# Attention by head pair in a one-core transformer kernel: two half-array matmuls side by side, index scores from stacked parts

## The chip, the core and the metric

The kernel runs on one core of a Trainium2 chip. TensorE (PE in the profile) does all matrix products and transposes; its weight loads stand apart as PEld. VectorE (DVE), ScalarE (ACT) and GpSimd (POOL) do the elementwise work, and SyncE (SP) issues most transfers. The metric is the device time of one execution in microseconds (us).

## The reference

Two transformer blocks over 512 tokens of width 1024, in fp32. Cut to what matters here:

```python
# block 1: FFN, then MLA attention (8 heads) and differential attention (4 heads of two halves), FFN, a gate
s = einsum('bhqd,bhkd->bhqk', q, k) * scale          # MLA, 96 dims a head, values 64 wide
a1 = softmax(q1 k1 * scale + bias); a2 = softmax(q2 k2 * scale + bias)   # halves of 64 dims
o = (a1 - lam * a2) @ v
# block 2, over 16 meta tokens and the 512: stick-breaking attention (8 heads) and sparse attention (8 heads)
s_idx = relu(einsum('bqhd,bkd->bqhk', qi, ki))       # 8 index heads of 64 dims share one key
score = einsum('bqh,bqhk->bqk', wi, s_idx)           # then the 128 best admissible keys of each query
p = softmax(q k * scale, selected keys); o = p @ v   # 8 heads, 64 dims, 64-wide values
# then a mixture of 32 experts (2 per token) and a last norm
```

## The kernel before

**Layout.** Activations lie transposed, 128 features on the partitions and 512 tokens along the free axis (`T`; 528 with the meta tokens, `TK`). A pair of 64-dim heads shares one tile: head `e` of the pair is rows `64e` to `64e+63`. Most products are made from two parts of each operand: `HL` holds a high part and a low part in fp32r, and `mm3` makes a product of three matmuls (high by high, high by low, low by high). Attention weights and values are multiplied as plain fp32; each such matmul stands in the trace as two records.

**Stages.** In order of time: FFN 1, the mixer of block 1 (`block1`), FFN 2, the gate, the mixer of block 2 (`mixer2`, `mixer2_out`), the experts. In both mixers two generators are merged by `merge`: `attention()` and a stream of projection tasks, each of which loads a weight tile (`wload`: transfer, high part on ACT, low part on DVE or POOL in turn) and runs a chain of full-array products. Each `yield` carries a planned cost, and `merge` advances whichever generator is behind in the ratio of its two weights (100 to 135 in block 1, 115 to 180 in block 2). `need(key)` holds attention back until the stream has come to a task. The planned costs set the program order alone; the library's scheduler then orders each engine's instructions by priority and by when it takes their inputs to be ready. `next_to` pins an instruction behind the one traced before it on its engine. PE takes its instructions in the order so made.

**Attention in block 1.** `diff_s(h)` (score matmuls of the two halves of a head, in rows 0 to 63 and 64 to 127, for four blocks of 128 queries; DVE adds the bias and takes the minimum, L751, ACT the exponential, L755), `diff_o`, `mla_s(p)`, and `mla_o(p)`: for each of four key blocks and both heads of pair `p`, `cols` transposes the weights into PSUM and copies them to `at`, and one fp32 matmul (L869) adds into 64 rows of `po`.

**Attention in block 2.** `idx` makes the index scores: `prep(c)` rotates and splits the queries of two heads, `products(c)` multiplies them by the index key `ki`, whose 64 rows lie twice on the partitions; ACT takes the relu, DVE the weighted sum. `sb_a`, `sb_b` and their kin are the stick-breaking heads, `rank` steps the top-k on DVE; none of these is touched. `ds_s(p)` makes the scores of the sparse heads, one head after the other, over 144, 272, 400 and 528 keys (the last in two segments of 264), and `ds_o(p)` their products with the values, for five key blocks and each head in turn (L1505, L1515).

**Buffers.** PSUM has three pools that rotate: `G` (3 banks, accumulation), `PS` (3, scores), `PT` (2, transposes). In SBUF, `U` takes from a pool of 41 or, for names in `SHORT` (`at`, `sb`, `sbb` among them), of 27 buffers.

## Time and profile before

| | us |
|---|---|
| median of 3 runs | 2258.01 (2257.05 to 2260.27) |
| the profiled execution, its own time | 2262.45 |
| its span, first to last instruction | 2260.6 |
| mean granted TensorE clock in it | 0.975 of 2.4 GHz |

The span is that of one execution taken by the profiler; times of stretches are read from it, in us from its start. A group's "busy" is the union of its instructions, and ends of matmuls are modelled, so the cost of a matmul is read here from its start to the start of the next one.

### The profile page before, as it was taken

To read this page: it belongs to the slowest core of one execution; us is meant where nothing else is said; L and a number is where in the kernel's file an instruction comes from. 1 tells how busy PE (TensorE), PEld (TensorE's weight loads), DVE (VectorE), ACT (ScalarE), POOL (GpSimd) and SP (SyncE) were. 2 spreads that over 40 slices of the span, in tenths; PEclk is the share of its full clock that TensorE was granted. 3 is DMA by queue.
4 is the path that set the end of the run, shared out by engine and by line. 5 is a ranking of instruction groups with operands and counts; after the bars stand their busy time and mean duration, and the time that the engine had idled before them with its cause. 6 is when DMAs were issued, how large, how long until landed. Compare 5 with 4: busy or idle time off the path is not lost.

```text
span 2260.6 us, 25763 instructions
## 1 busy us (share of the span) xinstructions
PE 2188.1 (97%) x10265; PEld 1544.3 (68%) x10265; DVE 1013.9 (45%) x1715; ACT 708.3 (31%) x1173; POOL 516.9 (23%) x336
## 2 busy tenths in 40 slices
PE   8999999999899999999989899999999999999997
PEld 6888888776655788888776777755788544455543
DVE  4323235556664542433574896543363232233322
ACT  4222224444443422222342555533232111111112
POOL 3323234232220432323432344210122000000000
PEclk9999999998999999999987999999999999999999
DMA  4333224210010233232321111111534799999993
GB/s 158 98 96 94 93 93 147 71 60 29 10 47 19 89 98 94 94 93 94 119 75 47 38 38 38 42 38 47 214 100 168 296 407 410 413 403 407 413 407 156
DMA packets 67838, 330.74 MB, mean 146 GB/s; under 512 B 7792, under 2 KB 8960, under 8 KB 43648
## 3 DMA queue, kind: packets, MB, share of 16 engines
q1 hardware_dynamic: 66848, 327.45, 39.1%
q8 instruction: 83, 1.36, 0.2%
q10 hardware_dynamic: 864, 1.57, 0.2%
q14 instruction: 43, 0.35, 0.0%
HBM read 326.90 MB, written 2.10 MB: 146 GB/s over the span
## 4 chain that ended last, share of the span: by engine, by line
PE 87%; DVE 7%; ACT 2%; issue 2%; POOL 1%; DMA 1%; SPq 0%; DVEq 0%; POOLq 0%; ACTq 0%
PE psg L391 10%; PE psg L392 10%; PE psg L393 10%; PE pss L1678 10%; PE psg L1678 7%; PE pss L391 5%; PE pss L393 5%; PE pss L392 5%; PE pst L1678 4%; PE pst L392 4%; PE pst L391 4%; PE pst L393 4%; PE psg L869 1%; PE psg L1515 1%; PE pst L1035 1%
## 5 line engine op out<-in xcount | busy, mean ns | idle before, releaser
L372 ACT ACTIVATE whl<-wraw 128x1024 fp32r<-128x1024 f32 (+1 forms) x227 | 237.1, 1044 | 664.6 <-PE psg L393 258.0
L375 POOL TENSOR_TENSOR whl<-wraw,whl 128x1024 fp32r<-128x1024 f32 (+1 forms) x114 | 271.3, 2379 | 685.8 <-ACT whl L372 509.4
L375 DVE TENSOR_TENSOR whl<-wraw,whl 128x1024 fp32r<-128x1024 f32 (+1 forms) x113 | 156.9, 1388 | 55.2 <-ACT whl L372 55.1
L1978 POOL TENSOR_TENSOR fr<-fv,mhalf 128x1 f32<-128x1 f32 x4 | 2.2, 546 | 518.7 <-DVE fv L1977 516.2
L1678 PE MATMUL pss<-mw,xe 128*64 128x512 f32 x512 | 115.3, 592 | 0.0
L1678 PE MATMUL pss<-mw,hT 128*64 128x512 f32 x480 | 108.0, 603 | 0.6 <-ACT hT L1856 0.5
L1678 PE MATMUL psg<-mw,xe 128*64 128x512 f32 x480 | 108.1, 592 | 0.0
L497 POOL TENSOR_TENSOR t<-t,t 128x512 f32<-128x512 f32 x44 | 58.4, 1326 | 216.8 <-DVE t L496 199.3
L496 DVE TENSOR_TENSOR t<-pss,rb_f 128x512 f32<-128x512 f32 x44 | 30.4, 691 | 163.2 <-PE pss L393 163.2
L524 DVE SCALAR_TENSOR_TENSOR h<-pst,h 128x512 f32<-128x512 f32 x48 | 33.2, 691 | 135.1 <-PE pst L393 135.0
L1838 DVE SCALAR_TENSOR_TENSOR mt<-pss,sc,mt 128x512 f32<-128x512 f32 x16 | 12.0, 750 | 178.5 <-PE pss L1678 178.5
L1951 DVE TENSOR_TENSOR h<-h,psg 128x512 f32<-128x512 f32 x120 | 81.1, 685 | 22.7 <-PE psg L1678 22.7
L1678 PEld LDWEIGHTS pss<-mw,xe 128*64 128x64 f32 x512 | 36.8, 137 | 73.1 <-issue 73.1
L1678 PEld LDWEIGHTS psg<-mw,xe 128*64 128x64 f32 x480 | 34.4, 137 | 68.1 <-issue 65.0
L387 DVE SCALAR_TENSOR_TENSOR yel<-pss,sc,yeh 128x512 fp32r<-128x512 f32 x32 | 24.0, 751 | 122.0 <-ACT yeh L386 122.0
L1678 PEld LDWEIGHTS pss<-mw,hT 128*64 128x64 f32 x480 | 33.5, 138 | 63.9 <-issue 59.3
L1678 PE MATMUL pst<-disp,uhh 128*128 128x256 f32 x256 | 69.6, 295 | 2.9 <-DVE disp L1756 2.9
L1678 PE MATMUL pst<-disp,uhl 128*128 128x256 f32 x256 | 67.9, 289 | 0.0
L413 POOL TENSOR_TENSOR acc<-acc,sq 128x512 f32<-128x512 f32 x34 | 53.4, 1572 | 46.2 <-ACT sq L412 42.5
L1678 PEld LDWEIGHTS pst<-disp,uhh 128*128 128x128 f32 x256 | 50.4, 197 | 17.6 <-issue 13.5
L1837 ACT ACTIVATE mt<-psg,sc 128x512 f32<-128x512 f32 x16 | 11.0, 687 | 157.1 <-PE psg L1678 134.2
L386 ACT ACTIVATE yeh<-pss,sc 128x512 fp32r<-128x512 f32 x32 | 22.0, 688 | 115.6 <-PE pss L1678 103.3
(880 smaller groups left out, 5770.3 us busy)
## 6 DMA issues: line engine op xcount, KB each, us to landing
mw<-in_w SPq DMA_DIRECT2D x188, 1024.0 KB, 9.4
wraw<-in_w_gu SPq DMA_DIRECT2D x87, 512.0 KB, 3.5
wraw<-in_w_d SPq DMA_DIRECT2D x48, 512.0 KB, 3.5
wraw<-in_w2A SPq DMA_DIRECT2D x38, 512.0 KB, 3.4
wraw<-in_w_inA SPq DMA_DIRECT2D x16, 512.0 KB, 3.5
wraw<-in_w_out SPq DMA_DIRECT2D x8, 512.0 KB, 3.6
wraw<-in_w_pg SPq DMA_DIRECT2D x8, 512.0 KB, 3.6
wraw<-in_w_up SPq DMA_DIRECT2D x8, 512.0 KB, 3.5
```

Source lines behind the costliest of these rows:

```text
L372: nc.scalar.activation(hl[:, 0, :n], raw[:, :n], AF.Copy)
L375: e.tensor_sub(hl[:, 1, :n], raw[:, :n], hl[:, 0, :n].bitcast(F32))
L387: nc.vector.scalar_tensor_tensor(low, src, scale, hi.bitcast(F32), op0=OP.mult, op1=OP.subtract)
L391: mm(ps, whi, xhi, start=first, stop=False)
L392: mm(ps, whi, xlo, start=False, stop=False)
L393: mm(ps, wlo, xhi, start=False, stop=last)
L413: (eng or nc.gpsimd).tensor_add(acc, acc, t)
L496: nc.vector.tensor_tensor(t2, pu, rb, op=OP.mult)
L497: nc.gpsimd.tensor_tensor(t2, t1, t2, op=OP.mult)
L524: nc.vector.scalar_tensor_tensor(self.h[m], py, 0.5, self.h[m], op0=OP.mult, op1=OP.add)
L1678: return self.next_to(nc.tensor.matmul(*args, **kw))
L1951: self.nc.vector.tensor_tensor(self.h[m], self.h[m], ps, op=OP.add)
```

## The change

The scores of a head pair, which were two `mm3` one after the other, become `mm3_pair`: six matmuls that alternate between the two halves of the partitions, pinned one behind the other, into two `PS` banks. The value products of `mla_o` and `ds_o`, which came one by one as their `at` was copied, are gathered: `mla_o` makes four `at` and then issues the four matmuls together, and `ds_o` does so with two, from a new pool of two buffers (`AT`). Both order the two heads' matmuls next to each other, in the left and the right 64 columns of the array. The index scores no longer use half the rows: `prep` puts the high part of a head's 64 rows and its low part on the other 64 rows of one tile, so that one full-height matmul makes two of the products, and two of them (against the high and the low part of `ki`) make all, with low by low added. Planned costs change with it.

```diff
@@ -24,6 +24,7 @@
...
 NG, NS, NT, NA, NB, NW, NMA, NMB = 3, 3, 2, 41, 27, 3, 7, 5
+NAT = 2
 NX, NU = 4, 0
@@ -259,7 +260,7 @@
...
                 self.setup()
-                with tc.tile_pool(name="ub", bufs=NB, side="right") as self.ub:
+                with tc.tile_pool(name="at", bufs=NAT, side="right") as self.pa, tc.tile_pool(name="ub", bufs=NB, side="right") as self.ub:
                     self.block1()
@@ -278,6 +279,9 @@
         return (self.ub if name in SHORT else self.ua).tile([P, w], dt, name=name, tag="u")
+    def AT(self):
+        return self.pa.tile([P, 512], F32, name="at", tag="at")
     def HL(self, name, w=512):
@@ -396,6 +400,18 @@
         return self.tc.keep_in_program_order(ins)
+    def mm3_pair(self, ps, w, x):
+        mm = self.nc.tensor.matmul
+        first = True
+        for a, b in ((0, 0), (0, 1), (1, 0)):
+            for e in (1, 0):
+                ins = mm(ps[e], w(e, a), x(e, b), start=a + b == 0, stop=a == 1)
+                if not first:
+                    self.next_to(ins)
+                first = False
     def gemm(self, ps, w, xs, kc, o=0, stride=P, cols=slice(None)):
@@ -741,21 +757,21 @@
...
                 sm, es = [], []
-                for e in range(2):
-                    ps = self.PS()
-                    tk = slice(i * P, (i + 1) * P)
-                    r = slice(64 * e, 64 * e + 64)
-                    self.mm3(ps, q[r, 0, tk], q[r, 1, tk], k[r, 0, :], k[r, 1, :], True, True)
+                tk = slice(i * P, (i + 1) * P)
+                rows = [slice(64 * e, 64 * e + 64) for e in range(2)]
+                pss = [self.PS() for e in range(2)]
+                self.mm3_pair(pss, lambda e, a: q[rows[e], a, tk], lambda e, a: k[rows[e], a, :])
+                for e in (1, 0):
                     sb = self.U("sb")
                     mn = self.S("mn", 1)
-                    nc.vector.tensor_tensor_reduce(out=sb, in0=ps, in1=dist[i], op0=OP.add, op1=OP.min, scale=1.0,
+                    nc.vector.tensor_tensor_reduce(out=sb, in0=pss[e], in1=dist[i], op0=OP.add, op1=OP.min, scale=1.0,
                                                    scalar=3.0e38, accum_out=mn)
...
                     nc.scalar.activation(sb, sb, AF.Exp, bias=mn, scale=-(4.0 ** -(h + 1)), accum_out=s)
-                    sm.append(s)
-                    es.append(sb)
-                yield 1.3
+                    sm.insert(0, s)
+                    es.insert(0, sb)
+                yield 0.8
                 cf = self.S("cf", 1)
@@ -862,12 +878,20 @@
...
             vm = vd["m", p]
-            for j in range(4):
-                for e in range(2):
-                    at = self.U("at")
-                    self.cols(at, aa[e], j)
-                    mm(po[64 * e : 64 * e + 64], vm[:, j * P + 64 * e : j * P + 64 * e + 64], at, start=j == 0, stop=j == 3)
-                    yield 0.9
+            for j0 in (0, 2):
+                ats = []
+                for e in (0, 1):
+                    for j in (j0 + 1, j0):
+                        at = self.U("at")
+                        self.cols(at, aa[e], j)
+                        ats.append((e, j, at))
+                        yield 0.45
+                for n, m in enumerate((3, 1, 2, 0)):
+                    e, j, at = ats[m]
+                    ins = mm(po[64 * e : 64 * e + 64], vm[:, j * P + 64 * e : j * P + 64 * e + 64], at, start=n < 2 and j0 == 0, stop=n > 1 and j0 == 2)
+                    if n:
+                        self.next_to(ins)
+                yield 2.2
             rbh = self.U("rbh")
@@ -1258,7 +1282,10 @@
...
                 q = self.HL("qi")
-                self.split(q, y2)
+                for e in range(2):
+                    r, o = slice(64 * e, 64 * e + 64), slice(64 - 64 * e, 128 - 64 * e)
+                    nc.scalar.activation(q[r, e, :], y2[r], AF.Copy)
+                    nc.vector.tensor_sub(q[o, e, :], y2[r], q[r, e, :].bitcast(F32))
                 qi[c] = q
@@ -1268,18 +1295,18 @@
...
                         h = 2 * c + e
-                        r = slice(64 * e, 64 * e + 64)
                         rl = self.U("relu", TK)
...
                             ps = self.PS()[:, : oe - o]
-                            self.mm3(ps, q[r, 0, tk], q[r, 1, tk], ki[r, 0, o:oe], ki[r, 1, o:oe], True, True)
+                            for s in range(2):
+                                mm(ps, q[:, e, tk], ki[:, s, o:oe], start=s == 0, stop=s == 1)
                             nc.scalar.activation(rl[:, o:oe], ps, AF.Relu)
...
                             nc.vector.scalar_tensor_tensor(mk[i], rl[:, :n], wc, mk[i], op0=OP.mult, op1=OP.add)
-                        yield n * 0.00128
+                        yield n * 0.0009
             qi = {}
@@ -1464,27 +1491,26 @@
...
             sm = self.S("smm", 8)
-            al_ = []
-            for e in range(2):
-                r = slice(64 * e, 64 * e + 64)
-                al = []
-                for i in (3, 2, 1, 0):
-                    n = NK[i]
-                    tk = slice(i * P, i * P + P)
-                    sb = self.U("sbb", TK)
-                    mn = None
-                    for o, e_ in segs(n):
-                        ps = self.PS()[:, : e_ - o]
-                        self.mm3(ps, qp[r, 0, tk], qp[r, 1, tk], kh[r, 0, o:e_], kh[r, 1, o:e_], True, True)
+            al_ = [[], []]
+            rows = [slice(64 * e, 64 * e + 64) for e in range(2)]
+            for i in (3, 2, 1, 0):
+                n = NK[i]
+                tk = slice(i * P, i * P + P)
+                sb = [self.U("sbb", TK) for e in range(2)]
+                mn = [None, None]
+                for o, e_ in segs(n):
+                    pss = [self.PS()[:, : e_ - o] for e in range(2)]
+                    self.mm3_pair(pss, lambda e, a: qp[rows[e], a, tk], lambda e, a: kh[rows[e], a, o:e_])
+                    for e in (1, 0):
                         m2 = self.S("mn", 1)
-                        nc.vector.tensor_tensor_reduce(out=sb[:, o:e_], in0=ps, in1=mk[i][:, o:e_], op0=OP.add, op1=OP.min,
-                                                       scale=1.0, scalar=3.0e38 if mn is None else mn, accum_out=m2)
-                        mn = m2
-                    nc.scalar.activation(sb[:, :n], sb[:, :n], AF.Exp, bias=mn, scale=-1.0,
+                        nc.vector.tensor_tensor_reduce(out=sb[e][:, o:e_], in0=pss[e], in1=mk[i][:, o:e_], op0=OP.add, op1=OP.min,
+                                                       scale=1.0, scalar=3.0e38 if mn[e] is None else mn[e], accum_out=m2)
+                        mn[e] = m2
+                for e in (1, 0):
+                    nc.scalar.activation(sb[e][:, :n], sb[e][:, :n], AF.Exp, bias=mn[e], scale=-1.0,
                                          accum_out=sm[:, 2 * i + e : 2 * i + e + 1])
-                    al.insert(0, sb)
-                    yield n * 0.00128
-                al_.append(al)
+                    al_[e].insert(0, sb[e])
+                yield n * 0.0014
             r1 = self.S("r1m", 8)
@@ -1493,27 +1519,31 @@
...
             for j in (4, 0, 1, 2, 3):
-                for e in range(2):
-                    pc = slice(p * P + 64 * e, p * P + 64 * e + 64)
-                    pr = slice(64 * e, 64 * e + 64)
+                ats = []
+                for e in (0, 1):
                     pt = self.PT()
-                    at = self.U("at")
+                    at = self.AT()
                     if j == 4:
...
                         nc.vector.tensor_copy(at[:NM], pt[:NM])
-                        mm(po[pr], vh[4][:NM, pc], at[:NM], start=True, stop=False)
-                        yield 0.8
-                        continue
-                    nq = T - j * P
-                    for i in range(j, 4):
-                        nc.tensor.transpose(pt[:, (i - j) * P : (i - j + 1) * P], al_[e][i][:, NM + j * P : NM + j * P + P], self.ident)
-                    if e:
-                        nc.vector.tensor_copy(at[:, :nq], pt[:, :nq])
+                        ats.append((vh[4][:NM], at[:NM], 0))
                     else:
-                        nc.scalar.copy(at[:, :nq], pt[:, :nq])
-                    mm(po[pr, j * P :], vh[j][:, pc], at[:, :nq], start=False, stop=j == 3)
-                    yield 0.9 - 0.2 * j
+                        nq = T - j * P
+                        for i in range(j, 4):
+                            nc.tensor.transpose(pt[:, (i - j) * P : (i - j + 1) * P], al_[e][i][:, NM + j * P : NM + j * P + P], self.ident)
+                        if e:
+                            nc.vector.tensor_copy(at[:, :nq], pt[:, :nq])
+                        else:
+                            nc.scalar.copy(at[:, :nq], pt[:, :nq])
+                        ats.append((vh[j], at[:, :nq], j * P))
+                    yield 0.45 - 0.1 * (j % 4)
+                for e in (1, 0):
+                    v, at, o = ats[e]
+                    ins = mm(po[64 * e : 64 * e + 64, o:], v[:, p * P + 64 * e : p * P + 64 * e + 64], at, start=j == 4, stop=j == 3)
+                    if e == 0:
+                        self.next_to(ins)
+                yield 1.3 - 0.3 * (j % 4)
             rbh = self.U("rbh")
...
```

## Rows read from the trace of the kernel before

**Rows 1.** The page: the span, and busy time of each engine.

```profile
span 2260.6 us, 25763 instructions
PE 2188.1 (97%) x10265; PEld 1544.3 (68%) x10265; DVE 1013.9 (45%) x1715; ACT 708.3 (31%) x1173; POOL 516.9 (23%) x336
```

**Rows 2.** Stretches: length, busy PE, PEld, DVE, ACT, POOL, clock, DMA share, GB/s.

```profile
385.00:505.00 120.00, 119.14 (x570) 90.69 (x569) 61.08 (x154) 52.68 (x97) 34.48 (x21) 1.00 0.23 76
505.00:605.00 100.00, 88.51 (x380) 61.24 (x379) 65.66 (x156) 49.49 (x106) 30.65 (x24) 0.88 0.09 27
605.00:745.00 140.00, 133.50 (x598) 84.01 (x597) 85.44 (x138) 61.01 (x121) 27.57 (x17) 1.00 0.11 34
1195.00:1275.00 80.00, 75.52 (x329) 56.10 (x328) 48.29 (x77) 27.47 (x59) 14.37 (x8) 0.77 0.11 40
1275.00:1385.00 110.00, 100.20 (x588) 81.08 (x587) 101.23 (x266) 57.79 (x109) 49.57 (x56) 0.97 0.12 39
1440.00:1600.00 160.00, 159.84 (x684) 99.69 (x683) 69.30 (x161) 59.18 (x125) 20.96 (x10) 0.99 0.13 43
```

**Rows 3.** Timeline of PE: differential scores, two halves that happened to alternate (start, duration).

```profile
458.08 0.50 PE L392 MATMUL pss<-dkl,dqh 64*128 64x512 f32 x1
458.09 0.49 PE L391 MATMUL pss<-dkh,dqh 64*128 64x512 f32 x1
458.42 0.39 PE L393 MATMUL pss<-dkh,dql 64*128 64x512 f32 x1
458.43 0.39 PE L392 MATMUL pss<-dkl,dqh 64*128 64x512 f32 x1
458.66 0.39 PE L393 MATMUL pss<-dkh,dql 64*128 64x512 f32 x1
458.98 0.44 PE L1035 MATMUL pst<-ident,ad 128*128 128x128 f32 x2
```

**Rows 4.** Timeline of PE: one half's three score matmuls alone.

```profile
459.57 0.49 PE L391 MATMUL pss<-dkh,dqh 64*128 64x512 f32 x1
...
460.45 0.33 PE L1035 MATMUL pst<-ident,ad 128*128 128x128 f32 x1
```

**Rows 5.** Timeline of PE: one fp32 value product (two records) and what follows it.

```profile
702.75 1.07 PE L869 MATMUL psg<-at,vm 128*64 128x512 f32 x2
703.75 0.66 PE L445 MATMUL pst<-ident,bce 128*128 128x128 f32 x4
```

**Rows 6.** The chain of waits, experts: eight fp32 products (16 records), alternating column halves.

```profile
2000.86 3.43 PE pss L1678 x16
```

**Rows 7.** Timeline of PE: sparse scores of one head, 528 keys, then 400.

```profile
1512.85 0.38 PE L391 MATMUL pss<-khh,qph 64*128 64x264 f32 x1
...
1513.77 0.50 PE L391 MATMUL psg<-xs2h,whl 128*128 128x512 f32 x1
...
1515.68 0.45 PE L391 MATMUL pss<-khh,qph 64*128 64x400 f32 x1
...
1516.42 0.49 PE L391 MATMUL psg<-xs4h,whl 128*128 128x512 f32 x1
```

**Rows 8.** Stretches of the index scores, columns as in rows 2.

```profile
1210.50:1237.80 27.30, 26.48 (x69) 16.79 (x68) 11.24 (x17) 6.76 (x17) 1.65 (x2) 0.50 0.10 37
1258.20:1268.50 10.30, 10.30 (x52) 9.67 (x51) 8.56 (x22) 6.80 (x14) 1.29 (x1) 0.50 0.00 0
```

**Rows 9.** Timeline of PE: full-height matmuls of 264 columns, one behind the other.

```profile
1250.03 0.28 PE L391 MATMUL psg<-xs6h,whl 128*128 128x264 f32 x1
1250.15 0.28 PE L392 MATMUL psg<-xs6l,whl 128*128 128x264 f32 x1
```

**Rows 10.** DVE: timeline of one split; group of score passes (busy, mean ns).

```profile
1207.28 2.44 DVE L384 TENSOR_TENSOR qil<-yqi,qih 128x512 fp32r<-128x512 f32 x1 [1.54 <-ACT qih L383]
...
L751 DVE CUSTOM_DVE_ANT_0 sb<-pss,dist 128x512 f32<-128x512 f32 x32 | 21.9, 683 | 0.5 <-PE pss L393 0.4
```

**Rows 11.** Waits of PE, 385 to 745 us: total, times, longest.

```profile
PE pss L391 <- DVE mn L751: 2.1, 1, 2.1
```

## The prediction, made before the changed kernel ran

> **What bounds the kernel now.** I read the page first, then a table of stretches, then the timeline of PE inside each stretch that the change touches. The page has PE busy for 2188.1 of 2260.6 us and no other engine for half of it [rows 1]. The stretches show where that holds for the attention [rows 2]. From 385 to 505, the differential heads, PE is busy for 119 of 120 us, and from 1440 to 1600, the sparse heads, for all of 160, with DVE and ACT far below: a microsecond off PE's queue is there a microsecond off the end, as long as the projections that fill it last. From 505 to 605, where block 1 passes from differential to MLA heads, PE stands idle for 11.5 us and its clock averages 0.88: chains through DVE and ACT set part of that stretch. From 1195 to 1275, the index scores, PE is busy for 75.5 of 80 us, but at a mean clock of 0.77. From 1275 to 1385, the stick-breaking heads with the top-k, DVE is busy for 101 of 110 us; nothing of the change lies there. The experts and both FFNs, most of the span, aren't touched, so everything below is a sum over four stretches.
>
> **Scores of the differential heads.** One half's three matmuls, alone, hold PE from 459.57 to 460.45, 0.88 us: three times 0.23 us and some 0.2 us for going over to half-height matmuls and back [rows 4]. The trace shows the new form by luck: where the two halves alternate, their matmuls start 0.01 us apart, and five of the six take 0.90 us, from 458.08 to 458.98 [rows 3]. So six side by side cost what three cost now. There are 4 heads, 4 query blocks and 2 halves: 32 groups of 0.88 us are 28.2 us, 16 pairs of 0.90 us are 14.4 us. Some are interleaved already, so I take 13 us, not 13.8. If the halves did not run together, the gain would be 0; that is the lower bound.
>
> **Value products of MLA.** One fp32 product alone takes 1.00 us to the next start [rows 5]. In the experts, where the two column halves alternate, eight take 3.43 us, 0.43 us each [rows 6]; twice 0.43 from 1.00 leaves 0.14 us for entry and exit. Now 32 stand alone, 32.0 us. After, 8 groups of four cost 4 x 0.43 + 0.14 = 1.86 us, together 14.9 us. The gain is 17 us; transposes and copies of `at` stay as they are.
>
> **Value products of the sparse heads.** Per pair and head: two of 512 columns, then 384, 256 and 128. With 0.14 us fixed and 0.86 us per 512 columns, an estimate from [rows 5], that is 1.00 + 1.00 + 0.79 + 0.57 + 0.36 = 3.72 us, over 8 heads 29.8 us. A pair costs as much as one does alone, so half goes: 14.9 us, of which I take 14.
>
> **Scores of the sparse heads.** One head's 528 keys take 0.92 us and its 400 keys 0.74 us [rows 7]; shorter blocks scale to about 0.58 and 0.45 us. That is 2.69 us a head and block set, 21.5 us over 8; half is 10.8 us. The two segments of 528 now want four score banks where there are three, so some second pairs come apart; I take 10 us.
>
> **Index scores.** Three half-height matmuls become two of full height, with no going over to another mode. At the spacing of [rows 9], 0.12 us for 264 columns, one head costs 2 x (2 x 0.12 + 0.18 + 0.12 + 0.11) = 1.3 us, 10.4 us for 8; by [rows 7] the old form costs 21.5 us if every head stands alone. Heads already overlap in this stretch, so I take 7 of these 11 us. The larger item is the clock: for 27.3 and 10.3 us it was granted 0.50, the 1.2 GHz level, with PE busy for 36.8 us of it [rows 8]; at 2.4 GHz that work takes half, so 18.4 us are lost now. Half-height matmuls fill much of these stretches; before the first, PE had waited for a split on DVE that took 2.44 us [rows 10]. After, the matmuls are full-height, and the same split is two DVE instructions, so the first drop stays and the way back should be shorter. The bounds are 0 and 18 us; I take 11, nearer to the upper because the work that stays is dense. The added split instructions, one more of about 0.7 us on DVE, as a DVE pass over 512 columns takes [rows 10], and one on ACT for each of 4 head pairs, hide behind the products of the pair before, all but the first; uncovered, 1.4 us each.
>
> **What is added as waits.** A pair starts when the later of its two operands is there. Behind it on PE's queue stand the next projection matmuls, and for those wait a `G` bank's evacuation on DVE and the next weight tile. The new two-buffer pool makes the copy of key block j+1 wait for the pair of block j: about 2 us of chain per block, 20 blocks, 40 us inside a stretch of 160 that has projections to fill it. Planned costs move: attention is emitted sooner against the stream, whose weight loads on SP keep their order and only come later against attention. The new pool lies beside the one that the experts' first weight tiles will reuse; they wait for the end of attention as before.
>
> **Given back.** In 505 to 605 the chains stay; a third of the differential gain falls there, and thinner PE work means longer idle: 6 us. In 605 to 745, 3 us. In the index stretch DVE, 48 of 80 us now, comes close to PE: 3 us. In the stick-breaking stretch, where DVE sets the time, a little less projection work lies under it: 3 us. Together 15 us, an estimate between 5 and 35.
>
> **Sum.** 13 + 17 + 14 + 10 + 7 + 11 = 72 us off PE, less 15: 57 us. The profiled execution took 2262.45 us, 1.85 us more than its span; so 2205 us for one like it, and, against the median of 2258.01, 2201 us. That is 2.5% faster. About 0.2%, 4.5 us, can be told from no change.
>
> **A rule against it.** The scores of a query block are emptied from PSUM by DVE, and the two halves of one block need 2 x 0.68 us there for the pass alone [rows 10], more than the 0.90 us that PE will need [rows 3]. The Trainium skill, "TensorEngine Tiling (Array Packing)", section "Performance Considerations", says that tiling speeds up TensorE but not the emptying of PSUM, which may become the bottleneck. By that rule the first rival below would be the outcome.
>
> **Rivals.**
> *Evacuation takes over.* Within a burst of differential attention DVE then sets the step, and PE's gain counts only where projections fill it. For it: DVE is at 66 of 100 us in 505 to 605 and PE idles already [rows 2]. Against it: over all of 385 to 745 DVE has 212 of 360 us. Then block 1 keeps 10 of 30 us, the index stretch 7 of 18, the sparse heads 20 of 24: 37 us, 2221 us. Chance 0.18.
> *The clock comes back wholly and little is given back.* 72 + 7 - 5 = 74 us, 2184 us. For it: dense full-height work; against it, every new gap on PE. Chance 0.08.
> *The pairs don't run together,* because the order made for PE puts other work between them. Then only the index part is left, 18 less 3: 2243 us. Against it: rows 3 and 6 show pairs where nothing stands between. Chance 0.05.
> *Slower: pairs wait on PE's own queue.* A pair takes two of three `PS` banks, so the next waits for DVE, and pinned in order it stops all behind it. There are 16 + 8 + 20 + 20 = 64 groups. The longest wait of this kind now is 2.1 us, once [rows 11]. At 2.1 us each that is 134 us against 72: 2320 us. It decides from 72 / 64 = 1.1 us a group. Against it: projections can stand between two pairs, and only the second segment of 528 keys follows at once. Chance 0.07, of which 0.02 within 0.2%.
>
> **How the numbers follow.** My forecast has 0.62, with its own range of 2186 to 2216 us. To leave no more than 2 in 10 out, the range takes in the first rival and the better clock down to 2182 us; upwards to 2234 us. Faster: 0.62 + 0.18 + 0.08 + 0.05 = 0.93; the slower rival gives 0.02 within 0.2% and 0.05 slower.
>
> **What would show it.** Score matmuls of `dkh` and `khh` starting in twos within 0.02 us; `L869`'s successor in groups of four in about 1.9 us; PE busy in the mixer of block 1 less by about 30 us; the clock below 1 in the index stretch for well under 37 us; the sparse stretch some 22 us shorter with PE still full. Wrong would be: new PE waits on DVE or on `at` above 20 us in total, more stretches at 0.50 than before, or lone half-height matmuls.

## The result

The changed kernel takes 2198.54 us (median of 4 runs, 2197.20 to 2201.16) against 2258.65 us for the kernel before beside it: ratio 0.9735, 95% interval 0.9721 to 0.9749, so 2.65% faster. Later, on two chips, it took 2200.20 and 2199.73 us. The profiled execution took 2201.16 us and its span is 2199.3 us. The forecast was 2201 us.

The page's span, busy times of all engines, and chain of waits, after:

```profile
span 2199.3 us, 25719 instructions
...
PE 2115.3 (96%) x10225; PEld 1520.7 (69%) x10225; DVE 1012.4 (46%) x1719; ACT 707.7 (32%) x1177; POOL 517.4 (24%) x336
...
PE 83%; DVE 9%; ACT 3%; issue 2%; POOL 1%; DMA 1%; SPq 0%; DVEq 0%; ACTq 0%; POOLq 0%
```

PE is busy for 72.8 us less than in [rows 1], and the span is 61.3 us shorter: PE stands idle for 84.0 us in all (2199.3 - 2115.3) where it was 72.5. The other engines do the same work. The stretches that answer to [rows 2], moved to where the same work now lies; the first three make up the attention of block 1:

```profile
385.00:505.00 120.00, 117.09 (x579) 90.39 (x577) 61.29 (x155) 52.85 (x98) 35.66 (x22) 0.99 0.24 77
505.00:600.00 95.00, 83.60 (x397) 59.70 (x394) 65.36 (x161) 51.96 (x114) 29.65 (x23) 0.87 0.09 28
600.00:721.00 121.00, 111.92 (x578) 79.95 (x577) 83.20 (x133) 57.45 (x114) 27.95 (x17) 1.00 0.13 40
1170.00:1230.00 60.00, 53.87 (x291) 44.83 (x289) 48.42 (x75) 30.33 (x64) 15.16 (x8) 0.97 0.16 53
1230.00:1340.00 110.00, 99.17 (x578) 83.36 (x577) 103.06 (x269) 56.77 (x108) 50.52 (x55) 0.94 0.12 39
1395.00:1530.00 135.00, 132.63 (x680) 87.75 (x679) 69.34 (x164) 58.65 (x128) 18.54 (x10) 1.00 0.16 48
```

The largest single change is in the fourth line: the index scores, which took 80 us at a mean clock of 0.77, take 60 us at 0.97. In the sparse heads (last line) PE is still nearly full; in stick-breaking (fifth line) DVE is still the engine nearest to full, 103 of 110 us.

Where the 61 us came from, by starts in the timeline of PE: the second FFN of block 1 starts 24.5 us earlier than before (836.3 to 811.9), the first index matmul 22.6 (1207.4 to 1184.7), the first stick-breaking matmul 45.9 (1271.1 to 1225.1), the first output projection of block 2 62.7 (1675.3 to 1612.6), the end 61.4. So block 1 gave about 24 us and the index stretch 23; 17 more lie between the first stick-breaking matmul and the first output projection, and the FFNs and the experts gave nothing. Within these 17, the first sparse score matmul is 40.1 us earlier (1444.6 to 1404.5): 5.8 us were lost ahead of it, in and behind stick-breaking, and the sparse heads gave 22.6.

**The pairs.** Two score pairs of a differential head in PE's timeline, after:

```profile
419.17 0.51 PE L410 MATMUL pss<-dkh,dqh 64*128 64x512 f32 x2
419.51 0.40 PE L410 MATMUL pss<-dkl,dqh 64*128 64x512 f32 x2
419.74 0.39 PE L410 MATMUL pss<-dkh,dql 64*128 64x512 f32 x2
419.97 0.39 PE L410 MATMUL pss<-dkh,dqh 64*128 64x512 f32 x1
420.29 0.50 PE L395 MATMUL psg<-xs4h,whl 128*128 128x512 f32 x1
420.63 0.39 PE L396 MATMUL psg<-xs4l,whl 128*128 128x512 f32 x1
...
421.64 0.49 PE L410 MATMUL pss<-dkh,dqh 64*128 64x512 f32 x1
421.65 0.72 PE L410 MATMUL pss<-dkl,dqh 64*128 64x512 f32 x2
421.99 0.60 PE L410 MATMUL pss<-dkh,dql 64*128 64x512 f32 x2
422.23 0.39 PE L410 MATMUL pss<-dkh,dqh 64*128 64x512 f32 x1
```

The first pair runs in three twos, 0.80 us to the fourth row. That fourth row is the first matmul of the *next* pair, alone: it starts at once, so its bank, the third, was free. Its partner starts at 421.64, as the second of the two DVE passes that empty the pair before ends (the row below, 420.97 and 0.68); until then projections come between (420.29). The next pair runs staggered, and behind it the first matmul of the one after stands alone again (422.23). Of 48 twos of the differential heads 43 start within 0.03 us of each other, of 60 of the sparse heads 51.

```profile
420.97 0.68 DVE L767 CUSTOM_DVE_ANT_0 sb<-pss,dist 128x512 f32<-128x512 f32 x1
```

**The value products of MLA** come in groups of four (eight records); to the next start one group takes 1.86 us:

```profile
693.73 1.94 PE L891 MATMUL psg<-at,vm 128*64 128x512 f32 x8
695.59 0.50 PE L397 MATMUL psg<-oT7h,whl 128*128 128x512 f32 x1
```

**The clock of the index stretch.** What answers to [rows 8]: the two stretches at 0.50 are 3.4 and 6.8 us long, and between them, with PE busy for 38.6 of 44.4 us, the clock stays at 1.00. The second lies behind the last index matmul (1222.3), in stick-breaking.

```profile
1186.50:1189.90 3.40, 3.40 (x11) 3.19 (x12) 2.21 (x4) 1.72 (x4) 0.00 (x0) 0.50 0.13 53
1189.90:1234.30 44.40, 38.55 (x232) 32.51 (x231) 39.24 (x67) 27.43 (x62) 10.67 (x7) 1.00 0.11 36
1234.30:1241.10 6.80, 5.96 (x19) 5.27 (x20) 6.66 (x16) 2.23 (x4) 2.39 (x3) 0.50 0.26 77
```

### The profile page after: what moved, and what is told of

Read it like the earlier page. It is cut to its first block, busy times and chain, and to the rows that moved or that the text cites. A ratio compares the mean times of both kernels' runs of the same rounds, so it can differ in the third digit from the quotient of the medians.

```text
span 2199.3 us, 25719 instructions
## 1 busy us (share of the span) xinstructions
PE 2115.3 (96%) x10225; PEld 1520.7 (69%) x10225; DVE 1012.4 (46%) x1719; ACT 707.7 (32%) x1177; POOL 517.4 (24%) x336
## 4 chain that ended last, share of the span: by engine, by line
PE 83%; DVE 9%; ACT 3%; issue 2%; POOL 1%; DMA 1%; SPq 0%; DVEq 0%; ACTq 0%; POOLq 0%
PE pss L1708 10%; PE psg L395 9%; PE psg L397 9%; PE psg L396 9%; PE psg L1708 8%; PE pss L395 4%; PE pss L397 4%; PE pss L396 4%; PE pst L1708 4%; PE pst L396 4%; PE pst L395 4%; PE pst L397 4%; PE pss L410 1%; PE pst L479 1%; PE pst L1713 1%
## 5 line engine op out<-in xcount | busy, mean ns | idle before, releaser
L1708 PE MATMUL pst<-disp,uhl 128*128 128x256 f32 x256 | 67.5, 288 | 0.0
L429 POOL TENSOR_TENSOR acc<-acc,sq 128x512 f32<-128x512 f32 x34 | 53.5, 1573 | 46.2 <-ACT sq L428 42.5
```

What stands on the lines that cost most here:

```text
L429: (eng or nc.gpsimd).tensor_add(acc, acc, t)
L1708: return self.next_to(nc.tensor.matmul(*args, **kw))
```

## The experiments

One number is used throughout, the **time lost at 0.50** of a profiled execution: span x (1 - mean granted clock), what the span would be shorter by if PE set the time everywhere and always had 2.4 GHz. The third digit of the clock makes it uncertain by 1.1 us. What is left, span less this, is called the work below. All times are medians. The groups of runs were on different chips; the kernel before, beside each of them, took 2252.6 to 2260.2 us, and a ratio is to the one beside. The last three columns are of one execution each, and the lost time differs between executions: over all of them on record it is 49.5 to 61.1 us for the kernel before, while its work is 2198.7 to 2206.5 us. So differences in the column of lost time are safe only well above 5 us.

| kernel | us | span, clock of the profile | lost at 0.50 | work |
|---|---|---|---|---|
| before | 2258.65 | 2260.6, 0.975 | 56.5 | 2204.1 |
| changed (second profile) | 2200.20 | 2198.4, 0.982 | 39.6 | 2158.8 |
| only_index | 2239.27 | 2233.0, 0.984 | 35.7 | 2197.3 |
| only_values | 2222.22 | 2221.3, 0.978 | 48.9 | 2172.4 |
| only_scores | 2237.05 | 2233.8, 0.981 | 42.4 | 2191.4 |
| heads_in_turn | 2211.18 | 2202.2, 0.984 | 35.2 | 2167.0 |
| index_as_before | 2213.51 | 2211.7, 0.976 | 53.1 | 2158.6 |
| index_three | 2205.20 | 2203.3, 0.981 | 41.9 | 2161.4 |
| index_pair | 2210.80 | 2211.4, 0.977 | 50.9 | 2160.5 |
| four_banks | 2251.98 | 2250.5, 0.970 | 67.5 | 2183.0 |
| held_pairs | 2193.19 | 2193.9, 0.982 | 39.5 | 2154.4 |
| held_in_block1 | 2197.89 | 2197.9, 0.980 | 44.0 | 2153.9 |

**One part at a time.** Each takes the hunks of the change for that part and nothing else but the new, there partly unused, pool: `only_index` the stacked split and the two full-height matmuls; `only_values` the grouped products of `mla_o` and `ds_o`; `only_scores` `mm3_pair` in `diff_s` and `ds_s`.

> The kernel before with the index scores from stacked parts alone (the split into stacked parts, two full-height matmuls instead of three half-height ones). Theory A (the parts add up, each by what it takes off PE's queue where PE is full): about 20 us faster, 2238 us, of which most is the stretch at 0.50 that shrinks from 37 us to about 10 us, with the attention of block 1 as before. Theory B (the clock of the index stretch came back for another reason, because everything ahead of it had moved): the long stretch at 0.50 stays, and the gain is some 6 us, 2252 us.

Measured 2239.27 us, ratio 0.9925 (0.9897 to 0.9953). The stretch at 0.50 is gone, with no matmul ahead of it changed; what was the first of [rows 8] now runs at 1.00:

```profile
1207.00:1243.00 36.00, 31.49 (x185) 26.73 (x186) 31.35 (x47) 20.78 (x49) 8.37 (x5) 1.00 0.17 47
```

Theory A. By the table, 20.8 us of its gain are clock and 6.8 us work.

> The kernel before with the value products of the MLA heads and of the sparse heads grouped, and nothing else. Theory A: 16.7 us of MLA and 13.5 us of sparse products come off PE, 30 us, of which a few are given back as idle time ahead of the index stretch: 2230 us, between 2226 and 2236. Theory B (an evacuation by DVE or ACT sets the pace, and the products had been hidden behind copies of the attention weights): half of that or less, above 2240 us.

Measured 2222.22 us, ratio 0.9843 (0.9815 to 0.9870), below the range of theory A. Work gave 31.7 us, about what the products take less (30); the rest is clock by the table. Theory B, the rival of the evacuation, has nothing here.

> The kernel before with the scores of the differential and of the sparse heads by pair, and nothing else (the sparse value products take their copies from the new small pool, but one by one as before). Theory A: 9.4 and 7.0 us come off PE, 16 us, of which a little is lost again: 2245 us, between 2241 and 2250. Theory B (pairs wait on PE's own queue for a free score bank or for DVE): no gain or slower, 2256 us or more.

Measured 2237.05 us, ratio 0.9923 (0.9897 to 0.9949), a gain of 21 us and below theory A's range of times. By the table it is 12.7 us of work and 14.1 us of clock, but the profiled execution was its fastest; over all five the lost time is 42.4 to 56.1 us. No waiting of pairs on PE's queue made it slower.

The three parts gain 19, 36 and 21 us by their medians, 76 in all, where the whole change gained 60. The table shows why: in work they sum to 6.8 + 31.7 + 12.7 = 51.2 us against 45.3, nearly additive; in time lost at 0.50 they sum to 42.5 us against 16.9. Medians over all executions, each against the kernel before beside it, say the same with less spread: 2.1 + 29.0 + 12.3 = 43.4 us of work against 45.8, and 16.0 + 5.3 + 8.3 = 29.6 us lost at 0.50 against 14.7. So it looks as if each part alone recovered some of the same low stretches, which can be recovered only once.

**The heads in turn.** Everything as changed, but the alternation:

```diff
-        for a, b in ((0, 0), (0, 1), (1, 0)):
-            for e in (1, 0):
+        for e in (1, 0):
+            for a, b in ((0, 0), (0, 1), (1, 0)):
```

> The changed kernel, but in the pair of score matmuls the three matmuls of one head come first and then the three of the other; banks, pins, planned costs and all else are unchanged. Theory A (the two halves of the array run at the same time when their matmuls alternate): the 16 us that the scores gained are lost again, 2214 us, and score groups take 0.88 us a head instead of 0.90 us for both. Theory B (the gain of the scores comes from the new order and the new planned costs): within 4 us of the changed kernel, 2195 to 2203 us.

Measured 2211.18 us, 11 us above the changed kernel: theory A, a little smaller. One head alone now takes 0.87 us to the projection behind it (421.08 to 421.95), where a whole pair takes 0.90 us for both (419.41 to 420.31 in `held_pairs`, below). Summed from each start to the next start on PE, at most 1 us for each, all score matmuls take 43.8 us (before 48.9, changed 32.5). That is not all of the gain lost: some still overlap at the seam of the two heads, most of them in the sparse heads (17.0 us where the kernel before took 21.5). PE's timeline of two heads of this kernel:

```profile
421.08 0.49 PE L410 MATMUL pss<-dkh,dqh 64*128 64x512 f32 x1
421.41 0.39 PE L410 MATMUL pss<-dkl,dqh 64*128 64x512 f32 x1
421.64 0.39 PE L410 MATMUL pss<-dkh,dql 64*128 64x512 f32 x1
421.95 0.50 PE L395 MATMUL psg<-xs5h,whl 128*128 128x512 f32 x1
422.38 0.50 PE L410 MATMUL pss<-dkh,dqh 64*128 64x512 f32 x1
```

**The clock of the index stretch, three ways.** `index_as_before` undoes the index part in the changed kernel. `index_three` keeps the stacked parts but issues three full-height matmuls, counting the low part of the key twice. `index_pair` goes back to half-height matmuls, those of two heads alternating, and to the old split; the heads' weighted sum runs in another order.

The core of `index_three`, and then of `index_pair`:

```diff
-                            for s in range(2):
-                                mm(ps, q[:, e, tk], ki[:, s, o:oe], start=s == 0, stop=s == 1)
+                            for n_, s in enumerate((0, 1, 1)):
+                                mm(ps, q[:, e, tk], ki[:, s, o:oe], start=n_ == 0, stop=n_ == 2)
```

```diff
+                self.split(q, y2)
...
+                        pss = [self.PS()[:, : oe - o] for e in range(2)]
+                        self.mm3_pair(pss, lambda e, a: q[rows[e], a, tk], lambda e, a: ki[rows[e], a, o:oe])
```

> The changed kernel with the index scores and their split as they were before the change. Theory A (work adds up, but the time lost at 0.50 is shared: each part alone recovered some of the same low stretches): 7 us of matmul work come back and a stretch of 0.50 of about 20 to 27 us in the index part, 2215 to 2219 us in all; with the clock set aside (span less the time lost at 0.50), 6 to 8 us more than the changed kernel. Theory B (the parts add up in time as well): 2219 to 2221 us by the 19 to 21 us of the index part alone, with no such difference in what is lost at 0.50.

> The changed kernel with three full-height index matmuls instead of two; the third counts the low part of the key a second time. So the work of the index scores in matmuls is as it was before the change, but without half-height ones. Theory A (the half-height matmuls kept PE at 0.50 there): no stretch of 0.50 above 10 us in the index stretch, only the 7 us of the added matmuls are lost, 2205 us. Theory B (the clock came back because there is less index work, or none of it waits): a stretch of 0.50 of 20 us or more comes back, 2212 us or more.

> The changed kernel with the index scores as pairs of half-height matmuls of two heads, as in the other scores, and the old split; the heads' weighted sum runs in another order. Theory A (half-height matmuls keep the clock low, side by side or not): a long stretch of 0.50 comes back, 2207 us or more. Theory B (it is the half-filled array that keeps the clock low; pairs fill it): 0.50 stays as short as in the changed kernel, PE spends three starts on two heads instead of four, and the time is 2192 to 2199 us.

`index_as_before` took 2213.51 us, 13 us more than the changed kernel, a little less than theory A's range, and by the table all of the 13 us is clock (53.1 against 39.6 us lost; by medians of all executions 11 of them): the work, which I had expected to be 6 to 8 us more, is the same within the reading. The long stretch is back, as in [rows 8]; the matmuls saved by stacking are paid for by PE's idle time, 34.4 us from 1135 to 1700 us in the changed kernel and 28.9 us here. `index_three` took 2205.20 us, and no long stretch came back: theory A. So half as many index matmuls again leave the clock alone. `index_pair` took 2210.80 us, and two stretches of 10.2 us at 0.50 are there, though its index matmuls take PE 17.0 us from start to start, little more than the full-height ones (14.4): theory A again. The stretches of `index_as_before`, and then those of `index_pair`:

```profile
1189.00:1216.30 27.30, 26.49 (x69) 16.74 (x69) 11.24 (x17) 6.87 (x17) 1.74 (x2) 0.50 0.10 38
1236.80:1247.00 10.20, 10.20 (x52) 9.57 (x51) 8.45 (x22) 6.80 (x14) 1.28 (x1) 0.50 0.00 1
```

```profile
1188.70:1198.90 10.20, 10.20 (x31) 6.38 (x31) 5.47 (x11) 2.33 (x7) 1.11 (x1) 0.50 0.04 15
1216.00:1226.20 10.20, 10.20 (x44) 7.43 (x40) 5.82 (x11) 3.24 (x9) 0.00 (x0) 0.50 0.10 40
```

PE has no gap in the last two, and still the clock stays at 0.50; with full-height matmuls it had gaps and 1.00. Half-height pairs don't lower it everywhere: among the projections of the sparse heads it is 1.00. `index_pair` changes the split too, so its 10 us are not a measure of the matmuls' height alone. More waiting for the split is not the reason, though. From the first to the last index matmul of the kernel before, the changed kernel, `index_three` and `index_pair`:

```profile
1207.40:1264.10 56.70, 52.22 (x212) 36.29 (x211) 31.65 (x47) 18.41 (x45) 8.84 (x5) 0.71 0.08 28
1184.70:1222.60 37.90, 33.37 (x188) 28.53 (x189) 31.76 (x47) 21.36 (x50) 8.66 (x5) 0.95 0.15 48
1186.70:1225.90 39.20, 35.50 (x215) 30.74 (x216) 32.30 (x48) 21.78 (x50) 8.66 (x5) 1.00 0.17 48
1184.40:1234.90 50.50, 47.10 (x236) 32.57 (x235) 31.29 (x48) 18.85 (x46) 10.05 (x6) 0.80 0.14 42
```

PE is idle for 4.5, 4.5, 3.7 and 3.4 us of it, at clocks of 0.71, 0.95, 1.00 and 0.80. All profiles here agree: the five kernels with half-height index matmuls have 0.71 to 0.80 in this stretch, the nine others 0.95 or 1.00. What no run shows is that half-height matmuls alone do it. In `index_pair` the last one starts at 1193.3 of the first stretch at 0.50 and at 1221.5 of the second, and full-height matmuls fill the rest; and `four_banks` (below), behind a wait of 3.82 us, has 10.2 us at 0.50 with PE busy throughout and full-height matmuls alone:

```profile
396.80:407.00 10.20, 10.20 (x33) 8.66 (x32) 0.92 (x5) 1.32 (x4) 0.00 (x0) 0.50 0.07 27
```

**The changed kernel once more.**

> The changed kernel once more, unaltered, beside the three that follow and the kernel before: every theory expects 2198 us, within 4 us. It gives the reading against which the next three stand, and shows whether the 13 us that its experts lost at 0.50 in the profile belong to it (then again above 10 us) or to that one execution (then about 6 us, as in the runs of single parts).

Measured 2200.20 us. From the output projections of block 2 to the end its profile lost 11 us at 0.50, that of the result 14, the three runs of single parts 7. So most of it belongs to the changed kernel, and some 3 us differ between executions.

**Another bank for the scores.**

```diff
-NG, NS, NT, NA, NB, NW, NMA, NMB = 3, 3, 2, 41, 27, 3, 7, 5
+NG, NS, NT, NA, NB, NW, NMA, NMB = 2, 4, 2, 41, 27, 3, 7, 5
```

> The changed kernel with four score banks and two projection banks instead of three and three. Theory A (with three banks the first matmul of the next pair takes the one free bank alone, and the pair runs staggered): nearly all 108 pairs then run side by side, the scores take 28 us of PE instead of 32.5, and the time falls to about 2194 us if two projection banks are enough. Theory B (projections need the third bank: with two, PE waits for the evacuation between column groups all through the kernel): slower than the changed kernel, 2205 us or more, although the pairs run side by side.

Measured 2251.98 us, 52 us above the changed kernel. Theory B, and far larger than I had put it; nor do nearly all pairs run side by side (86 of 108 twos, fewer than the 94 with three banks). The first stretch of the attention shows it: PE is busy for 110.4 of 120 us (117.1 with three projection banks), its clock is 0.89, and DVE is busy for less, not more.

```profile
385.00:505.00 120.00, 110.36 (x480) 80.48 (x479) 55.17 (x143) 43.25 (x81) 26.50 (x16) 0.89 0.22 67
505.00:600.00 95.00, 87.63 (x379) 62.02 (x378) 49.86 (x134) 42.88 (x86) 27.01 (x20) 0.84 0.11 34
```

PE's idle time is 101.4 us (2250.5 - 2149.1) against 83.7, and 27.9 us more are lost at 0.50: the new gaps cost their length, and most likely the clock behind them. Projections do wait for a bank that DVE has to empty (L395, for `pgt`, `y` and `h`: 12.0 us against 2.7), as theory B has it, but that is only part of the new idle time.

**Pairs that wait for both banks.** The first matmul of a pair gets a dependence on the evacuation that frees its partner's bank; `held_in_block1` does so in `diff_s` alone.

```diff
+                elif self.emptied is not None:
+                    self.tc.add_manual_dep(ins.ins, self.emptied, mybir.DependencyInfo(mybir.DependencyClass.Sync, mybir.DependencyReason.ANTI), reason="pair")
```

> The changed kernel with one wait more: the first matmul of a score pair also waits until DVE has emptied one bank of the pair before it, so that it doesn't start alone in the third, free bank. Theory A (the lone first matmuls, some 28 in 108 pairs, are why the scores gained 16 us and not the 23 us of the forecast): the score matmuls take 4 to 6 us less of PE, 27 to 29 us in all, and the time is 2194 to 2197 us. Theory B (the lone matmuls only fill time in which PE would wait for DVE anyway): the pairs run side by side, the projections that stood in between move, and the time stays at 2200 us, within 3 us.

Measured 2193.19 us (2189.93 to 2196.58), ratio 0.9708 (0.9691 to 0.9726). The pairs are whole: 47 of 48 and 60 of 60 twos, and the score matmuls take 29.8 us. In its timeline the pair at 419.41 is followed by six projections, and the next pair runs in twos as well:

```profile
419.41 0.50 PE L412 MATMUL pss<-dkh,dqh 64*128 64x512 f32 x2
419.75 0.39 PE L412 MATMUL pss<-dkl,dqh 64*128 64x512 f32 x2
419.99 0.39 PE L412 MATMUL pss<-dkh,dql 64*128 64x512 f32 x2
420.31 0.50 PE L397 MATMUL psg<-xs4h,whl 128*128 128x512 f32 x1
...
421.89 0.50 PE L412 MATMUL pss<-dkh,dqh 64*128 64x512 f32 x2
```

Its span is 4.5 us shorter than that of the changed kernel's second profile (2193.9 to 2198.4). Of these, 4.1 are there when the differential scores end (562.7 against 566.8), 1.2 of them ahead of the first score matmul, where the wait can't act yet; the sparse scores, 2 us shorter on PE, bring hardly any.

> The changed kernel, unaltered, on the chip of the next one: 2199 us, within 4 us.

> As held_pairs, but only the differential scores wait; the sparse scores stay as in the changed kernel, with their lone first matmuls. In the profile of held_pairs all the time gained had been gained when the differential scores ended, and the 2 us that the sparse score matmuls took less brought nothing. Theory A (so it is): 3 to 5 us below the changed kernel beside it, the lone matmuls of the sparse scores still there. Theory B (the sparse pairs had a share, or the gain of held_pairs was scatter): within 2 us of the changed kernel.

The changed kernel took 2199.73 us and `held_in_block1` 2197.89 us, ratios 0.9752 (0.9729 to 0.9774) and 0.9743 (0.9720 to 0.9767): theory B by its letter. In its profile it leads the changed kernel beside it by 4.2 us at the second FFN (810.5 to 814.8), but 1.7 of these are clock and only 1.4 were gained over the differential scores; and the profile of the result, without the wait, is there at 811.9. It gives 3 us back in stick-breaking, where it is at 0.50 for 17.0 us against 10.2. So the profiles alone don't size the wait. By the work of all five executions each (medians 2153.9 and 2158.3 us, no overlap) it is worth about 4 us, of which 2 are lost again to the clock (41.7 against 39.6 us); that `held_pairs` is the fastest version here rests on one group of 5 runs, with an interval that touches that of the changed kernel.

## Why the prediction was right, and where its terms were off

The total was right to 2.5 us: 60 us gained where 57 were forecast. PE's busy time fell by 72.8 us where the sum had 72, and 11.5 were given back where it had 15. That close it is partly luck: the scores gave 7 us less than their terms, the index stretch 8 more. What each gain rests on was right.

**Scores: too high.** 13 + 10 us were forecast. From start to start, the differential scores went from 27.4 to 18.0 us and the sparse ones from 21.5 to 14.5, 9.4 + 7.0 us. "Six side by side cost what three cost now" holds for a whole differential pair (0.90 us, `held_pairs`). A step that failed is the one on the banks: I saw that four banks would be wanted where there are three for the two segments of 528 keys, and took 0.8 us off for it, but the third bank starts the first matmul of the *next* pair alone in nearly every burst, in the differential heads too. `held_pairs`, without these, has 29.8 us instead of 32.5, so they are 2.7 of the 6.6 us missing. The rest are sizes. The scores took 48.9 us before, not the 49.7 of the terms. In `held_pairs` the differential pairs take 17.3 us where 15.2 were left, since one comes apart between projections (517.8 to 533.1) and one runs at 0.50 (1.6 us from 552.4); the sparse ones take 12.5 where 11.5 were left, since two segments of 264 keys by pair take 0.57 us each, and one head's two together had taken 0.92.

**Value products: right.** 17 + 14 us were forecast; MLA went from 31.6 to 14.9 us (a group takes the 1.86 us that the two rows gave), the sparse heads from 28.5 to 15.0.

**Index: right in kind, low in size.** 7 + 11 us less 3 given back were forecast; the stretch gave 23 us. The stretches at 0.50 shrank from 37.6 to 10.2 us, which is 13.7 us at the other level, near the upper bound of 18 rather than at my 11. Inside the changed kernel the clock is nearly the whole of it (`index_as_before`). It goes with the half-height form, not with the amount of work (`index_three`) nor with PE's idle time, which is 4.5 us before and after; whether by the matmuls alone or by the split that comes with them, no run separates. That the first products wait for the split was right: PE stands for 1.64 and 0.94 us before them, the two DVE instructions one behind the other.

```profile
1184.75 0.39 PE L1302 MATMUL pss<-kih,qih 128*128 128x264 f32 x1 [1.64 <-DVE qih L1288]
...
1186.43 0.57 PE L1302 MATMUL pss<-kih,qil 128*128 128x264 f32 x1 [0.94 <-DVE qil L1288]
```

What the split adds was wrong. I put the added DVE instruction at 0.7 us, after a score pass. That is its median, but at the first head pair, where PE waits, it took 1.65 us, behind the other's 2.44. And it doesn't hide behind the products of the pair before: PE waits at each of the four head pairs, 6.0 us in all where it waited 4.5 us before. The waits for the split in the changed kernel, and then in the kernel before:

```profile
PE pss L1302 <- DVE qih L1288: 5.1, 4, 2.1
PE pss L1302 <- DVE qil L1288: 0.9, 1, 0.9
```

```profile
PE pss L391 <- ACT qih L383: 2.8, 3, 1.1
PE pss L393 <- DVE qil L384: 1.7, 1, 1.7
```

**Given back: near.** 15 us were forecast; PE's idle time over the whole span grew by 11.5 us, 4.5 of them in block 1 (18.9 to 23.4 us over the three stretches) where I had 9, 1.7 in the index stretch and 1.0 in the stick-breaking one where I had 3 each, and 2.2 in the sparse one, where I had none. The order of attention against its projections also moved: 8 us of the 33 us that MLA's last product was earlier went to output projections that were left over, and 9 us in the sparse heads likewise. These move work and cost nothing.

**The rivals.** Nor did the clock come back wholly, and the pairs do run together (94 of 108 twos). Evacuation did not take over: in block 1 PE waited for the emptying of scores for 1.6 us in all, once, 2.1 us before [rows 11], and `only_values` and `only_scores` gained more than PE's share.

```profile
PE pss L410 <- DVE mn L767: 1.6, 1, 1.6
```

The rule of the Trainium skill, "TensorEngine Tiling (Array Packing)", section "Performance Considerations", which puts it for a speedup of four where a pair has two, thus doesn't set the time here. The Trainium skill, "TensorEngine Tiling (Array Packing)", section "Restrictions and Gotchas", says that row tiling raises the pressure on PSUM, since different row tiles write to different banks. The traces agree: that is what left some matmuls alone, for 2.7 us of the 7, and `four_banks` shows that the bank can't be taken from the projections here. The slower rival failed by its own condition: a pair that waits doesn't hold PE's queue, because the order puts projections between the lone matmul and its pair. "Lone half-height matmuls", which I named as a sign of being wrong, were there, about 28 of them; the other two signs were not. The signs for it came: in block 1 PE is busy for 28.5 us less (341.2 to 312.6), and the sparse heads are 22.6 us shorter.

**What stays open.** Why the low stretches outside the index part come and go with every shift of the work (17 us at 0.50 from 545 us on in the changed kernel; before, 3.4 us at 535 and 6.8 us at 552 and at 562) wasn't tried. `only_index`, with the same matmuls up to there as the kernel before, has 17 us at 548.

## What to carry to other kernels

Where PE is full, two half-array matmuls cost the time of one only if both can start at once. A wait for both banks on the pair's first matmul makes the pairs whole (107 of 108 twos), though its gain here, 2 and 7 us, is hardly clear of noise; taking the bank from the stream that fills PE's gaps cost 52 us. A form that fills all rows by stacking can be worth more through the clock than through the matmuls that it saves. When several parts each gain from the clock, test them together: their work adds up, their clock gains didn't.

## What was not expected of the hardware

Around half-height matmuls of two heads side by side, which together use all rows, the clock was at 0.50 for 10.2 us twice with PE busy throughout (`index_pair`), while it stayed at 1.00 with full-height ones and PE busy for 38.6 of 44.4 us (changed kernel). It isn't the form alone: behind a wait of 3.82 us, full-height matmuls ran at 0.50 for 10.2 us in `four_banks`, PE busy throughout as well. And the way between half-height and full-height matmuls costs on both sides: the projection behind a lone score matmul starts its successor 0.34 us later instead of 0.23 us (420.29 to 420.63), and the last half-height matmul before it takes 0.32 us instead of 0.23.
